# Two of four Strassen weight sums moved from VectorE to accumulating transfers

## The chip, the cores and the metric

One core of a Trainium2 chip runs the whole program. The metric is the device time of one execution in microseconds. The engines are TensorE (PE; its weight loads are listed apart as PEld), VectorE (DVE), ScalarE (ACT), GpSimd (POOL) and SyncE (SP). SP and POOL also issue transfers; in this kernel SP issues nearly all of them.

## The reference

Two decoder layers over 512 tokens of width 2048, all in float32. Layer A selects keys with an indexer and attends to them; layer B is stick-breaking attention over one shared K and V. Each mixer's output is gated, projected, added to the residual, normalised, and gets a gated per-layer embedding. What the change touches are two products at the start of layer B, the shared K/V and the queries:

```
def shared_kv(x, w_kv):
    b, s, _ = x.shape
    k, v = jnp.split(x @ w_kv, [KVW_B], axis=-1)
    return k.reshape(b, s, N_KV_B, HEAD_DIM), v.reshape(b, s, N_KV_B, HEAD_DIM)

def mixer_b(x, w_in, w_o, k, v):
    b, s, _ = x.shape
    q, gate = jnp.split(x @ w_in, [WIDTH_B], axis=-1)
    ...
    o = from_blocks(lax.map(block_fn, (to_blocks(q), starts)))
    return (o * jax.nn.silu(gate)) @ w_o
```

## The kernel before

Activations lie transposed, as 16 blocks of 128 rows by 512 tokens. Every matrix product runs on values split in two: a high part rounded by ScalarE (`XH`, `wh`, `sh`) and the rest, formed by VectorE (`XL`, `wl`, `sl`), so a product of two blocks is three matmuls (`mm3`, lines 134 to 136).

Weights stream through a ring of three `raw` tiles of 128 x 2 x 512. `units` lists every load in the order of use; `next_raw` fills the ring from SP and hands out the oldest tile. A tile is free again when the last split has read it. `Ahead(..., 2)` keeps the split parts two items ahead of TensorE, and `wh` and `wl` have three buffers each. K of layer B is a plain product (`kitems`, eight units of two k blocks, in order `PAIRS`). V and the four groups of queries are five Strassen products in Winograd's form (`strassen_items`, `gemm_s`, lines 325 to 389): each job halves the width (256 columns), the inner dimension (1024) and the tokens (256) and needs seven products. One unit is k block k and k block k + 8, and eight units make a job, so 40 units in all. Call the four quarters of a unit q0 (upper left), q1 (upper right), q2 (lower left), q3 (lower right). VectorE forms in `st` four sums of them:

```
s1 = q0 + q2
s2 = s1 - q1
s3 = q1 - q0
s4 = q3 - s2
```

Then for each half of 128 columns the three quarters q1 to q3 and the four sums are split (128 x 384 and 128 x 512), and one item of seven pairs goes to TensorE: 21 matmuls of 256 columns. When a job's seven products are complete, `combine` (the last job: `combine_last`) adds them up from PSUM into the four quarters of the output while the next job runs in the banks that come free. During the plain product for K, `first_chunk` builds the activation sums for Strassen and the plain splits of the activations (`xl`), and at its last k block calls `stream().prime()`, which prepares the first two Strassen items.

TensorE's instructions stay in the order of the code. The other engines' order is set by a scheduler with a simulated timeline, but each engine takes its own queue in order: an instruction that waits holds up all behind it. `paced` and `pinned` mark instructions that the scheduler must leave in program order.

In the names of the rows, `raw` is a loaded weight tile, `wh` and `wl` (and `sh`, `sl`) the split weights, `st` the weight sums, `xh` and `xl` split activations, `c3h` and `c3l` split activation sums, `E` and `f` storage for activations, `u` and `m` a combine's helper tile and the product banks.

Of the kernel before, what the change touches and what calls it, by code (L numbers as in the profile page):

```python
# [77 lines left out]
def trunk_kernel(  # L78
# [85 lines left out]
    def add_job(src, c0, n=512, nk=NK, strassen=False):  # L164
        if n <= 128:
            units.extend((src.rearrange("(k p) n -> p k n", p=128)[:, k : k + 8, c0 : c0 + n],) for k in (0, 8))
            return
        step = nk // 2
        for k in range(step):
            a, b = (k, k + step) if strassen else (2 * k, 2 * k + 1)  # L170
            units.append((src, a, b, c0, n))
# [4 lines left out]

    def next_raw():
        while sent[0] < len(units) and len(raws) < 3:
            raw = top.tile([128, 2, 512], F32, name="raw", tag="raw", bufs=3)
            unit = units[sent[0]]  # L180
            if len(unit) == 1:
# [42 lines left out]
    def weight_parts():  # L224
        return tuple(top.tile([128, 512], F32R, name=n, tag=n, bufs=3) for n in ("wh", "wl"))
# [99 lines left out]
    def strassen_items(widths, wp):  # L325
        units = [n for n in widths for _ in range(NK // 2)]

        def prepare(n):
            raw = next_raw()
            rows = n // 256  # L330
            q = raw.rearrange("p a (b n) -> p (a b) n", b=2)
            two = [q[:, i].rearrange("p (j c) -> p j c", j=rows) for i in range(4)]
            st = wp.tile([128, 4 * H], F32, name="st", tag="st", bufs=2)[:, : 2 * n]
            st = st.rearrange("p (j i c) -> p j i c", j=rows, i=4)
            dve.tensor_tensor(st[:, :, 0], two[0], two[2], ALU.add)
            dve.tensor_tensor(st[:, :, 2], two[1], two[0], ALU.subtract)
            return q, two, st

        ready = prepare(units[0])
        for u, n in enumerate(units, 1):  # L340
            q, two, st = ready
            s1, s2, s3, s4 = (st[:, :, i] for i in range(4))
            dve.tensor_tensor(s2, s1, two[1], ALU.subtract)
            dve.tensor_tensor(s4, two[3], s2, ALU.subtract)
            rows = n // 256
            for j in range(rows):
                wh = top.tile([128, 512], F32R, name="wh", tag="wh", bufs=3)
                wl = top.tile([128, 512], F32R, name="wl", tag="wl", bufs=3)
                sh = wp.tile([128, 4, 128], F32R, name="sh", tag="sh", bufs=3)
                sl = wp.tile([128, 4, 128], F32R, name="sl", tag="sl", bufs=3)  # L350
                qh, ql = (w.rearrange("p (b c) -> p b c", b=4)[:, 0:3] for w in (wh, wl))
                split(qh, ql, q[:, 1:4, j * 128 : (j + 1) * 128])
                split(sh, sl, st[:, j])
                if j == rows - 1 and u < len(units):
                    ready = prepare(units[u])
                yield [(qh[:, i], ql[:, i]) for i in range(3)] + [(sh[:, i], sl[:, i]) for i in range(4)]
# [31 lines left out]
    def combine(wp, M, dst):  # L388
# [9 lines left out]
        dve.tensor_tensor(u, m6, u, ALU.add)  # L398
        pinned[0] = False

        def onto(c):
            dve.tensor_tensor(c, c, u, ALU.add)

        def rest():
            dve.tensor_tensor(c22, c12, c21, ALU.add)
            dve.tensor_tensor(c12, m3, c12, ALU.add)
            dve.tensor_tensor(c21, c21, m4, ALU.subtract)

        paced(rest)
        return [lambda c=c: onto(c) for c in (c12, c21, c22)]  # L410

    def combine_last(wp, M, dst):
# [6 lines left out]
        for out, a, b, op in (  # L419
            (c11, m2, u, ALU.add),  # L420
            (u, m6, u, ALU.add),
# [911 lines left out]
```

## Time and profile before

| | us |
|---|---|
| median of 3 runs | 1889.02 (1888.74 to 1889.87) |
| span of the profiled execution, first to last instruction | 1886.3 |
| own time of the profiled execution beside its span | not listed by the page; the median of the runs is 2.7 above the span |
| Strassen stage, first to last of its matmuls | 1037 to 1242 |
| granted TensorE clock, mean | 0.999 |

The page lists, for each engine, busy time, share of the span and number of instructions; then groups of instructions by line, with mean nanoseconds of one and the idle time of the engine before them; then the waits by the instruction that ended them. Rows of single instructions give the start and the duration in us from the span's start; a bracket at their end gives the engine's idle time before and what ended it. A line L111 or L134 is that of a helper, so groups are told apart by their tiles.

### The profile page before, as it was taken

How to read it: one execution, taken by the hardware profiler on the slowest of the kernel's cores; microseconds unless marked ns; L12 is line 12 of the kernel's file. 1: busy time of each engine (PE TensorE's matmuls, PEld its weight loads, DVE VectorE, ACT ScalarE, POOL GpSimd, SP SyncE). 2: the span in 40 equal slices, each digit the busy share in tenths (PEclk: the TensorE clock that was granted, in tenths of full speed). 3: DMA queues.
4: the chain of work that ended last, by engine and by line, in shares of the span. 5: the costliest groups of instructions: out<-in, count | busy, mean ns of one | idle time of the engine just before them, and what ended most of it. 6: DMA issues, size and time to landing. Idle time of an engine off the chain costs nothing.

```text
span 1886.3 us, 25050 instructions
## 1 busy us (share of the span) xinstructions
PE 1872.6 (99%) x9229; PEld 1586.7 (84%) x9229; DVE 1218.9 (65%) x2384; ACT 928.1 (49%) x1690; POOL 28.4 (2%) x49
## 2 busy tenths in 40 slices
PE   9999999999999999999999999999999999999998
PEld 8898888888888888888888999988888888888887
DVE  5668879966556454675368788866656645567534
ACT  4446323355554432474245444468877743347422
POOL 0000000000000000000000000000100000000000
PEclk9999999999999999999999999999999999999999
DMA  6432333312222432333343333322122153242333
GB/s 185 137 115 64 101 91 99 101 56 68 67 68 60 162 114 78 123 101 103 121 130 116 103 100 113 102 90 72 63 68 68 60 186 100 74 129 89 123 101 112
DMA packets 110587, 189.22 MB, mean 100 GB/s; under 512 B 8240, under 2 KB 28208, under 8 KB 110464
## 3 DMA queue, kind: packets, MB, share of 16 engines
q1 hardware_dynamic: 110320, 187.33, 32.4%
q8 instruction: 72, 1.18, 0.3%
q14 instruction: 51, 0.42, 0.1%
q0 software_dynamic: 144, 0.30, 0.1%
HBM read 179.21 MB, written 8.39 MB: 99 GB/s over the span
## 4 chain that ended last, share of the span: by engine, by line
PE 96%; DVE 2%; ACT 1%; DMA 1%; issue 0%; SPq 0%; POOL 0%; DVEq 0%; POOLq 0%
PE g L134 12%; PE g L135 12%; PE g L136 12%; PE o L135 7%; PE o L134 7%; PE o L136 7%; PE m L134 3%; PE m L135 3%; PE m L136 3%; PE q L136 3%; PE q L134 3%; PE q L135 3%; PE z L1214 2%; PE k L136 2%; PE k L135 2%; PE k L134 2%
## 5 line engine op out<-in xcount | busy, mean ns | idle before, releaser
L111 ACT ACTIVATE wh<-raw 128x512 fp32r<-128x512 f32 (+3 forms) x684 | 396.4, 581 | 674.4 <-PE g L135 239.4
L111 DVE TENSOR_TENSOR wl<-raw,wh 128x512 fp32r<-128x512 f32 (+3 forms) x684 | 429.6, 629 | 429.9 <-ACT wh L111 415.1
L134 PE MATMUL g<-xh,wh 128*128 128x512 f32 x1024 | 403.9, 394 | 0.2
L135 PE MATMUL g<-xl,wh 128*128 128x512 f32 x1024 | 400.3, 391 | 0.6 <-DVE xl L111 0.6
L136 PE MATMUL g<-xh,wl 128*128 128x512 f32 x1024 | 399.9, 390 | 0.0
L134 PEld LDWEIGHTS g<-xh,wh 128*128 128x128 f32 x1024 | 192.8, 188 | 40.4 <-ACT sg L111 1.9
L136 PEld LDWEIGHTS g<-xh,wl 128*128 128x128 f32 x1024 | 192.3, 188 | 40.8
L135 PEld LDWEIGHTS g<-xl,wh 128*128 128x128 f32 x1024 | 192.5, 188 | 38.4 <-DVE xl L111 1.4
L136 PE MATMUL o<-xh,wl 128*128 128x512 f32 x512 | 199.4, 389 | 0.1
L134 PE MATMUL o<-xh,wh 128*128 128x512 f32 x512 | 199.2, 389 | 0.0
L135 PE MATMUL o<-xl,wh 128*128 128x512 f32 x512 | 199.2, 389 | 0.0
L136 PEld LDWEIGHTS o<-xh,wl 128*128 128x128 f32 x512 | 96.1, 188 | 20.6 <-DVE wl L111 0.7
L134 PEld LDWEIGHTS o<-xh,wh 128*128 128x128 f32 x512 | 96.1, 188 | 20.2 <-ACT wh L111 0.2
L135 PEld LDWEIGHTS o<-xl,wh 128*128 128x128 f32 x512 | 96.1, 188 | 20.0
L134 PE MATMUL q<-xh,wh 128*128 128x512 f32 x256 | 99.6, 389 | 0.0
L135 PE MATMUL q<-xl,wh 128*128 128x512 f32 x256 | 99.6, 389 | 0.0
L136 PE MATMUL q<-xh,wl 128*128 128x512 f32 x256 | 99.6, 389 | 0.0
L111 ACT ACTIVATE sh<-st 128x512 fp32r<-128x512 f32 x80 | 49.0, 628 | 79.7 <-PE m L135 42.5
L111 DVE TENSOR_TENSOR sl<-st,sh 128x512 fp32r<-128x512 f32 x80 | 54.4, 689 | 37.2 <-ACT sh L111 37.2
L111 DVE TENSOR_TENSOR xl<-f,xh 128x512 fp32r<-128x512 f32 x80 | 54.3, 686 | 11.4 <-ACT f L111 11.0
L111 ACT ACTIVATE wk<-z 128x512 f32<-128x512 f32 x80 | 47.1, 590 | 25.7 <-PE z L136 18.0
L135 PEld LDWEIGHTS q<-xl,wh 128*128 128x128 f32 x256 | 48.1, 188 | 10.0
(290 smaller groups left out, 3366.5 us busy)
## 6 DMA issues: line engine op xcount, KB each, us to landing
raw<-w_in_a SPq DMA_DIRECT2D x95, 512.0 KB, 3.7
raw<-w_in_b SPq DMA_DIRECT2D x64, 512.0 KB, 3.8
raw<-w_ple_gate SPq DMA_DIRECT2D x52, 512.0 KB, 3.7
raw<-w_o_a SPq DMA_DIRECT2D x24, 512.0 KB, 3.9
raw<-w_o_b SPq DMA_DIRECT2D x24, 512.0 KB, 3.8
raw<-w_kv_b SPq DMA_DIRECT2D x16, 512.0 KB, 3.8
raw<-w_ple_gate SPq DMA_DIRECT2D x24, 256.0 KB, 2.9
f<-xT SPq DMA_DIRECT2D x4, 1024.0 KB, 6.4
```

The source lines that it names most:

```text
L111: ins = method(*args, **kw)
L134: pe.matmul(out, a[0], b[0], start=start, stop=False)
L135: pe.matmul(out, a[0], b[1], start=False, stop=False)
L136: pe.matmul(out, a[1], b[0], start=False, stop=stop)
L1214: pe.matmul(z, m, p, start=False, stop=n == len(terms), skip_group_check=True)
```

## The change

A Strassen load is now a unit of its own kind, `(src, k, c0)`, which `load_sums` brings in by five transfers into a `raw` tile of 128 x 5 x 256. SP loads q0 twice, into slots 0 and 1, by one broadcast transfer, then q2 and q3 into slots 3 and 4, and q1 into slot 2. POOL then adds q1 onto slot 0 and q2 onto slot 1, by transfers that accumulate in the tile. So slot 0 is q0 + q1 and slot 1 is q0 + q2. Only additions are used: two of the seven operands and with them the products' combination change sign (`combine`, `combine_last`). VectorE still forms two sums, slot 1 + q1 and q3 + that. The split is dealt out anew: 128 x 640 from the tile (five slots), 128 x 256 from `st` (two sums). The ring has four `raw` tiles, and the list of K's plain units is written out since `add_job(..., strassen=True)` now makes the new kind. The scratch that POOL's transfers reserve is set to 4096 bytes per partition.

```
@@ add_job
+            if strassen:
+                units.append((src, k, c0))
+            else:
+                units.append((src, 2 * k, 2 * k + 1, c0, n))
@@
+    def load_sums(raw, src, k, c0):
+
+        rows = src.rearrange("(k p) n -> p k n", p=128)
+        left, right = slice(c0, c0 + 256), slice(c0 + 256, c0 + 512)
+        nc.sync.dma_start(raw[:, 0:2], rows[:, k : k + 1, left].broadcast_to([128, 2, 256]))
+        both = raw[:, 3:5].rearrange("p a n -> p (a n)")
+        nc.sync.dma_start(both, rows[:, k + 8, c0 : c0 + 512])
+        nc.sync.dma_start(raw[:, 2], rows[:, k, right])
+        pool.dma_start(raw[:, 0], rows[:, k, right], accum_op=ALU.add)
+        pool.dma_start(raw[:, 1], rows[:, k + 8, left], accum_op=ALU.add)
@@ next_raw
-        while sent[0] < len(units) and len(raws) < 3:
-            raw = top.tile([128, 2, 512], F32, name="raw", tag="raw", bufs=3)
+        while sent[0] < len(units) and len(raws) < 4:
+            raw = top.tile([128, 5, 256], F32, name="raw", tag="raw", bufs=4)
             unit = units[sent[0]]
+            if len(unit) == 3:
+                load_sums(raw, *unit)
+                raws.append(raw)
+                sent[0] += 1
+                continue
@@ strassen_items
-            dve.tensor_tensor(st[:, :, 0], two[0], two[2], ALU.add)
-            dve.tensor_tensor(st[:, :, 2], two[1], two[0], ALU.subtract)
...
-            dve.tensor_tensor(s2, s1, two[1], ALU.subtract)
-            dve.tensor_tensor(s4, two[3], s2, ALU.subtract)
...
+            st = wp.tile([128, 2, 256], F32, name="st", tag="st", bufs=2)
+            dve.tensor_tensor(st[:, 0], raw[:, 1], raw[:, 2], ALU.add)
+            return raw, st
+
+        ready = prepare()
+        for u in range(len(widths) * NK // 2 - 1, -1, -1):
+            raw, st = ready
+            dve.tensor_tensor(st[:, 1], raw[:, 4], st[:, 0], ALU.add)
+            for j in range(2):
+                cols = slice(j * 128, (j + 1) * 128)
+                q = tuple(w.rearrange("p (b c) -> p b c", b=5) for w in weight_parts(640))
+                t = tuple(wp.tile([128, 2, 128], F32R, name=n, tag=n, bufs=3) for n in ("sh", "sl"))
+                split(*q, raw[:, :, cols])
+                split(*t, st[:, :, cols])
+                if j and u:
+                    ready = prepare()
+                s3, s1, a11, a22, a12 = ((q[0][:, i], q[1][:, i]) for i in range(5))
+                s2, s4 = ((t[0][:, i], t[1][:, i]) for i in range(2))
+                yield a11, a22, a12, s1, s2, s3, s4
@@ combine
-        dve.tensor_tensor(u, m6, u, ALU.add)
+        dve.tensor_tensor(u, m6, u, ALU.subtract)
...
-            dve.tensor_tensor(c22, c12, c21, ALU.add)
-            dve.tensor_tensor(c12, m3, c12, ALU.add)
-            dve.tensor_tensor(c21, c21, m4, ALU.subtract)
+            dve.tensor_tensor(c22, c12, c21, ALU.subtract)
+            dve.tensor_tensor(c12, m3, c12, ALU.subtract)
+            dve.tensor_tensor(c21, m4, c21, ALU.add)
@@
-    add_job(w_kv_b, 0, strassen=True)
+    units.extend((w_kv_b, k, k + 8, 0, 512) for k in range(8))
@@
-    nc = _bacc.Bacc("TRN2", target_bir_lowering=False, num_devices=1)
+    nc = _bacc.Bacc("TRN2", target_bir_lowering=False, num_devices=1, dynamic_dma_scratch_size=4096)
```

The change also moves instructions, since the scheduler sets them anew. First VectorE's queue at the entry to the Strassen stage, while TensorE still works on K's last k blocks. Before (`wl` of 512 columns are K's last plain splits, `st<-raw` the first sums of a unit):

```order
L111 TENSOR_TENSOR wl<-raw,wh 128x512
L111 TENSOR_TENSOR st<-raw 128x2x128 x2
L111 TENSOR_TENSOR st<-st,raw 128x2x128
L111 TENSOR_TENSOR st<-raw,st 128x2x128
L111 TENSOR_TENSOR wl<-raw,wh 128x512
L111 TENSOR_TENSOR xl_94<-E_5554,xh_78 128x256
L111 TENSOR_TENSOR xl_97<-f_107,xh_81 128x512
L111 TENSOR_TENSOR xl_105<-f_109,xh_89 128x512
L111 TENSOR_TENSOR sl<-st,sh 128x512 x2
L111 TENSOR_TENSOR wl<-raw,wh 128x512
L111 TENSOR_TENSOR st<-raw 128x2x128 x2
```

Two rows on, in that queue, comes the first Strassen split (`wl` of 384 columns), and only after it the third unit's sums. The same place in the changed kernel, up to the first Strassen splits (`wl` of 640 columns):

```order
L111 TENSOR_TENSOR st<-raw 128x256
L111 TENSOR_TENSOR wl<-raw,wh 128x512
L111 TENSOR_TENSOR st<-raw,st 128x256
L111 TENSOR_TENSOR sl<-st,sh 128x256 x2
L111 TENSOR_TENSOR wl<-raw,wh 128x512
...
L111 TENSOR_TENSOR st<-raw 128x256
L111 TENSOR_TENSOR xl_105<-f_109,xh_89 128x512
L111 TENSOR_TENSOR wl<-raw,wh 128x512 x2
...
L111 TENSOR_TENSOR st<-raw 128x256
L111 TENSOR_TENSOR st<-raw,st 128x256
L111 TENSOR_TENSOR wl<-raw,wh 128x640 x2
```

The first sum (`st<-raw`) now stands ahead of the plain split that was before it (k block 12), and the first Strassen splits stand behind the third unit's first sum and the second unit's second sum.

Second, VectorE at the first change of job, where `combine` (into `E`, through `u`) frees the banks that TensorE's next products need. Before:

```order
L111 TENSOR_TENSOR wl<-raw,wh 128x384
L111 TENSOR_TENSOR st<-raw 128x2x128 x2
L111 TENSOR_TENSOR E_5554<-m_8866,u 128x2x256
L111 TENSOR_TENSOR st<-st,raw 128x2x128
L111 TENSOR_TENSOR u<-m_8867,u 128x512
```

And in the changed kernel:

```order
L111 TENSOR_TENSOR wl<-raw,wh 128x640
L111 TENSOR_TENSOR st<-raw,st 128x256
L111 TENSOR_TENSOR E_5556<-m_8885,u 128x2x256
L111 TENSOR_TENSOR u<-m_8886,u 128x512
L111 TENSOR_TENSOR E_5556<-E_5556 128x2x256
```

One sum instead of two stands right ahead of the first bank's addition, and none between the first and the second.

Third, POOL between the masks of layer A's scores (`am`; `trf` is a constant) and those of layer B (`wk`, `run`). Before:

```order
L622 AFFINE_SELECT trf<-trf 128x128
L701 AFFINE_SELECT am_124<-am_124 128x128
L701 AFFINE_SELECT am_125<-am_125 128x128
L701 AFFINE_SELECT am_126<-am_126 128x128
L1172 AFFINE_SELECT wk<-wk 128x512 x4
L1172 AFFINE_SELECT run<-run 128x512
```

In the changed kernel the transfers stand there, two for each of the 40 units:

```order
L710 AFFINE_SELECT am1_124<-am1_124 128x128
L710 AFFINE_SELECT am2_125<-am2_125 128x128
L710 AFFINE_SELECT am3_126<-am3_126 128x128
L187 DMA raw_8691<-w_kv_b 128x256
L188 DMA raw_8691<-w_kv_b 128x256
L187 DMA raw_8735<-w_kv_b 128x256
L188 DMA raw_8735<-w_kv_b 128x256
```

The first of each pair waits until SP's broadcast transfer of its tile has landed, and the next unit's pair waits behind it in POOL's queue.

More of the change, by code (lines that the diff above doesn't have):

```diff
@@ L169, in add_job @@
         for k in range(step):
-            a, b = (k, k + step) if strassen else (2 * k, 2 * k + 1)
-            units.append((src, a, b, c0, n))
+            if strassen:
+                units.append((src, k, c0))
+            else:
+                units.append((src, 2 * k, 2 * k + 1, c0, n))
     raws = deque()
@@ L222, in __next__, with weight_parts @@
             return self.waiting.popleft()
-    def weight_parts():
-        return tuple(top.tile([128, 512], F32R, name=n, tag=n, bufs=3) for n in ("wh", "wl"))
+    def weight_parts(n=512):
+        return tuple(top.tile([128, n], F32R, name=n_, tag=n_, bufs=3) for n_ in ("wh", "wl"))
     def plain_items(jobs):
@@ L325, in strassen_items, with prepare @@
     def strassen_items(widths, wp):
-        units = [n for n in widths for _ in range(NK // 2)]
-        def prepare(n):
+        def prepare():
             raw = next_raw()
[L330 to L334, printed above, removed]
-            dve.tensor_tensor(st[:, :, 0], two[0], two[2], ALU.add)
-            dve.tensor_tensor(st[:, :, 2], two[1], two[0], ALU.subtract)
-            return q, two, st
@@ L339, in strassen_items @@
[L339 to L342, printed above, removed]
-            dve.tensor_tensor(s2, s1, two[1], ALU.subtract)
-            dve.tensor_tensor(s4, two[3], s2, ALU.subtract)
[L345 to L356, printed above, removed]
+            st = wp.tile([128, 2, 256], F32, name="st", tag="st", bufs=2)
@@ L397, in combine, with onto @@
         dve.tensor_tensor(c11, m2, u, ALU.add)
-        dve.tensor_tensor(u, m6, u, ALU.add)
+        dve.tensor_tensor(u, m6, u, ALU.subtract)
         pinned[0] = False
-        def onto(c):
-            dve.tensor_tensor(c, c, u, ALU.add)
+        def onto(c, a, b, op):
+            dve.tensor_tensor(c, a, b, op)
         def rest():
-            dve.tensor_tensor(c22, c12, c21, ALU.add)
-            dve.tensor_tensor(c12, m3, c12, ALU.add)
-            dve.tensor_tensor(c21, c21, m4, ALU.subtract)
+            dve.tensor_tensor(c22, c12, c21, ALU.subtract)
+            dve.tensor_tensor(c12, m3, c12, ALU.subtract)
+            dve.tensor_tensor(c21, m4, c21, ALU.add)
         paced(rest)
-        return [lambda c=c: onto(c) for c in (c12, c21, c22)]
+        last = ((c12, c12, u, ALU.subtract), (c21, u, c21, ALU.subtract), (c22, c22, u, ALU.add))
+        return [lambda ops=ops: onto(*ops) for ops in last]
     def combine_last(wp, M, dst):
@@ L420, in combine_last @@
             (c11, m2, u, ALU.add),
-            (u, m6, u, ALU.add),
-            (c21, m7, u, ALU.add),
+            (u, m6, u, ALU.subtract),
+            (c21, u, m7, ALU.subtract),
             (c22, m5, c21, ALU.add),
             (c12, m5, u, ALU.add),
-            (c12, m3, c12, ALU.add),
+            (c12, m3, c12, ALU.subtract),
             (c21, c21, m4, ALU.subtract),
```

## The prediction

> **What bounds the kernel.** I read the page's header, its busy line and its chain first: they say which engine sets the end.
>
> ```profile
> span 1886.3 us, 25050 instructions
> PE 1872.6 (99%) x9229; PEld 1586.7 (84%) x9229; DVE 1218.9 (65%) x2384; ACT 928.1 (49%) x1690; POOL 28.4 (2%) x49
> PE 96%; DVE 2%; ACT 1%; DMA 1%; issue 0%; SPq 0%; POOL 0%; DVEq 0%; POOLq 0%
> ```
>
> TensorE is busy 1872.6 of 1886.3 us, so all that any change off TensorE can give back is 13.7 us. The change leaves the list of matmuls alone (their shapes, operands' widths and order stay), so its worth is what it does to these gaps. Next, the table of stretches over the Strassen stage, and the waits of TensorE's weight loads inside it.
>
> ```profile
> core 0: us, PE busy (x) PEld busy (x) DVE busy (x) ACT busy (x) POOL busy (x), PEclk, DMA share, GB/s
> 1036.90:1242.00 205.10, 204.22 (x1687) 202.52 (x1687) 160.75 (x342) 92.17 (x177) 0.00 (x0) 1.00 0.34 104
> PEld m L134 <- DVE f L111: 1.1, 3, 0.4
> PEld m L134 <- DVE u L111: 1.0, 4, 0.3
> PEld m L134 <- DVE E L111: 0.4, 1, 0.4
> ```
>
> The stage runs at a granted clock of 1.00 and TensorE is idle 205.10 - 204.22 = 0.88 us in it. VectorE, which the change relieves, is busy 160.75 us of 205.10, or 78%: it is not the bound. TensorE's only waits here are on combine's instructions at the four changes of job. 40 units share the stage, so one unit of weights lasts 205.1 / 40 = 5.13 us.
>
> **What is removed.** Per unit VectorE formed four sums of 128x256; two remain.
>
> ```profile
> L111 DVE TENSOR_TENSOR st<-raw 128x256 f32<-128x256 f32 x80 | 30.2, 419 | 4.3 <-DMA raw<-w_kv_b 4.2
> L111 DVE TENSOR_TENSOR st<-raw,st 128x256 f32<-128x256 f32 x40 | 16.9, 422 | 0.8
> L111 DVE TENSOR_TENSOR st<-st,raw 128x256 f32<-128x256 f32 x40 | 16.7, 418 | 0.0
> ```
>
> 160 sums cost 30.2 + 16.9 + 16.7 = 63.8 us; 80 go, so 80 x 0.42 = 33.6 us leave VectorE, and its share of the stage falls to about (160.75 - 33) / 205 = 62%. The splits are only dealt out differently: per half unit 128x384 + 128x512 before, 128x640 + 128x256 after, 896 columns both times.
>
> ```profile
> L111 DVE TENSOR_TENSOR wl<-raw,wh 128x384 fp32r<-128x384 f32 (+1 forms) x81 | 44.7, 555 | 6.3 <-ACT wh L111 6.3
> L111 DVE TENSOR_TENSOR sl<-st,sh 128x512 fp32r<-128x512 f32 x78 | 53.1, 689 | 37.2 <-ACT sh L111 37.2
> ```
>
> 128 columns more cost 0.689 - 0.555 = 0.134 us, so I estimate the 640-wide split at 0.82 us: 0.82 + 0.42 = 1.24 against 0.555 + 0.689 = 1.24. ScalarE's copies keep their columns too. The combining instructions change signs and operand order, not number or size. All of this lies under TensorE. The one piece of it on the path is at the job changes, where VectorE reaches combine with fewer sums queued ahead: of the 0.88 us I take half, -0.4 us; the ends are 0 and -0.9.
>
> **What is added: transfers.** Per unit SP issued one 512 KB load; now it issues three (256, 256, 128 KB), and POOL two accumulating ones of 128 KB. Issues first. An SP issue takes 0.37 us (rows below), so 1.1 us per 5.13 us unit, and what is queued behind on SP is the next unit's load, which has to wait for its buffer anyway. POOL has no work at all in the stage (0.00 above), and its next instruction after the scores of layer A waits over a thousand microseconds, so nothing queues behind the two issues of 0.55 to 0.71 us.
>
> ```profile
> POOL wk L1172 <- DVE wk L111: 1155.3, 7, 1063.1
> 1.35 0.71 POOL L141 DMA_DIRECT2D lnc<-ln_c  x1 [0.34 <-issue]
> 2.04 0.55 POOL L582 DMA_DIRECT2D rc<-rope_c  x1
> ```
>
> Bandwidth: 512 KB per unit makes a DMA share of 0.34. The plain 640 KB would make 0.34 x 640/512 = 0.43. The accumulating 256 KB would add 0.17 at the price of a plain byte, and 0.34 at twice that (the destination is read as well), so 0.60 to 0.77. The engines fill up only if an accumulated byte costs over (1 - 0.43) / 0.17 = 3.4 plain ones.
>
> **What is added: a longer way from a free buffer to its first sum.** This decides. No row shows an accumulating transfer; the nearest in the list of issues (KB each, median us from issue to landing) are:
>
> ```profile
> raw<-w_kv_b SPq DMA_DIRECT2D x16, 512.0 KB, 3.8
> raw<-w_ple_gate SPq DMA_DIRECT2D x24, 256.0 KB, 2.9
> posi<-pos POOLq DMA_DIRECT2D x1, 256.0 KB, 5.5
> lnc<-ln_c POOLq DMA_DIRECT2D x1, 32.0 KB, 3.0
> rc<-rope_c POOLq DMA_DIRECT2D x1, 2.0 KB, 4.2
> ```
>
> Call L the time from a buffer's release until the second accumulation has landed: 2.9 (SP's 256 KB) + 0.71 (POOL's first issue) + the landing of the second. For that I take 4.2, the middle of POOL's three rows, since 128 KB lies between 32 and 256: L = 7.8 us. The low end takes 3.0 (L = 6.6). The high end takes twice 5.5, as if destination and source were read one after the other (L = 14.6). Before, release to sum was 3.7: the rows below show a `wl` ending at 1019.93 and the sum starting at 1023.58.
>
> [...]
>
> In the steady stage this is covered. With four buffers a freed one is wanted three units later, 3 x 5.13 = 15.4 us, against 2 x 5.13 = 10.3 us with three. L = 7.8 leaves 7.6 us; even 14.6 fits. The tight place is the entry, where VectorE takes its instructions in order and a sum that waits for its transfer holds up splits that TensorE needs.
>
> ```profile
> 1015.01 0.68 DVE L111 TENSOR_TENSOR wl<-raw,wh 128x512 fp32r<-128x512 f32 x1
> 1015.72 0.37 SPq L198 DMA_DIRECT2D raw<-w_kv_b  x1
> 1019.24 0.68 DVE L111 TENSOR_TENSOR wl<-raw,wh 128x512 fp32r<-128x512 f32 x1
> 1019.96 0.37 SPq L198 DMA_DIRECT2D raw<-w_kv_b  x1
> 1021.48 0.69 DVE L111 TENSOR_TENSOR wl<-raw,wh 128x512 fp32r<-128x512 f32 x1
> 1023.58 0.76 DVE L111 TENSOR_TENSOR st<-raw 128x256 f32<-128x256 f32 x2 [1.41 <-DMA raw<-w_kv_b]
> 1032.25 0.56 DVE L111 TENSOR_TENSOR wl<-raw,wh 128x384 fp32r<-128x384 f32 x1 [0.39 <-ACT wh L111]
> 1034.89 0.76 DVE L111 TENSOR_TENSOR st<-raw 128x256 f32<-128x256 f32 x2 [2.08 <-DMA raw<-w_kv_b]
> 1037.16 0.28 PE L134 MATMUL m<-xh,wh 128*128 128x256 f32 x1
> L134 PE MATMUL k<-xh,wh x64: 389/389/389, 993.6 to 1036.5; 128*128 128x512 f32 x64
> ```
>
> Before, the first unit's load went out at 1019.96, on the release of its third-last predecessor; with four buffers it goes out one unit of the plain job earlier, at 1015.7. That is a lead of 4.3 us, against L - 3.7 = 4.1 us more to wait: the two cancel. Now follow the changed order on VectorE. The first sum can run at 1015.7 + L, which is 1023.5 (before: 1023.58). Behind it stand the plain splits `wl` of k blocks 12 and 13. TensorE begins block n at 993.6 + 2.72 n (64 groups to 1036.5), so at 1026.2 and 1028.9; the splits are done about 1.0 and 3.6 us after the sum starts, at 1024.5 and 1027.1. The second of them frees the third unit's buffer, whose sum runs at 1015.7 + L + 3.6 + L = 1034.9. That is where it ran before (1034.89), but then the first Strassen split was already through, at 1032.25; in the new order it stands behind this sum and one more. It ends 1.6 us later (0.34 + 0.42 + 0.82), at 1036.5. TensorE wants its low part in its third matmul, at 1037.4. The margin is 0.9 us, and the entry stalls by 1020.9 + 2L - 1037.4 = 2L - 16.5 us if that is positive: from L = 8.25 on, twice, since two transfers stand one behind the other. At L = 7.8 it is 0; at 6.6 it is 0; at 14.6 it is 12.7 us.
>
> **Other moves.** The fourth buffer lets every load of the kernel start earlier, and ScalarE's and VectorE's orders shift in places. TensorE's waits show what that could touch:
>
> ```profile
> PE z L1214 <- ACT sh L111: 3.7, 1, 3.7
> PE spun L156 <- DVE xl L111: 2.0, 1, 2.0
> ```
>
> The 3.7 us after the stage hang on ScalarE's queue, whose order there is the same in both kernels; the 2.0 us are the start, before any load matters. I put 0 on both, with 1.5 us either way for small shifts.
>
> **Sum.** The page gives the span and no other time of the profiled execution; the median of the runs, 1889.02, lies 2.7 us above the span, and I keep that. 1886.3 - 0.4 + 0 + 0 = 1885.9 us of span, or 1888.6 us. A change under 0.2% (3.8 us) I count as no change; the three runs spread by 1.1.
>
> **Rivals.** *Late accumulations at the entry* (slower): VectorE in order behind a sum whose accumulation lands late. It passes 0.2% when 2L - 16.5 - 0.4 is over 3.8, so from L = 10.4, a landing over 6.8 us after issue. For it: no accumulating transfer has been timed, and POOL's 256 KB took 5.5. Against it: that one ran beside SP's first loads, and half the bytes go here. At the high end: 1889.0 + 12.7 - 0.4 = 1901.3 us. Chance 13%.
>
> [...] Chance of a decisive one 3%. [...]
>
> *Transfers become the bound* (slower): at five plain bytes for an accumulated one the share is 0.43 + 0.85 = 1.28, the stage 28% or 57 us longer, about 1946 us. For it only that the price is unknown. Chance 4%.
>
> *A true gain*: over 3.8 us would need the 3.7 us wait to vanish with all of the 0.88, or the shifts in order to remove what I do not see: 1885 or below. Chance 5%. That the sums stay on VectorE is excluded by the orders: 80 rows fewer there, 80 transfers on POOL.
>
> **How the numbers follow.** No change 75%, at 1888.6 us, by itself within 1886.5 and 1892.8; slower 13 + 3 + 4 = 20%; faster 5%. The range runs from 1886.5, which leaves the faster cases below it, to 1898, which takes in the entry's stall up to L = 13 (2 x 13 - 16.5 - 0.4 = 9.1 above 1889.0) and leaves about a third of the first slow rival and the whole of the third outside: some 15% in all.
>
> **What would show it.** Right: 80 `st` rows of about 0.42 us on VectorE, busy near 128 us in the stage; the POOL transfers land in 3 to 5 us; the stage stays at 205 us with TensorE's idle under 1 us. Wrong: a wait of TensorE on `wl` or `wh` at about 1037 (entry), a DMA share near 1 with a longer stage (bandwidth), POOL issues well over 0.7 us (descriptors), or a wait of TensorE at another place that the new orders made.

## The result and the profile after

The changed kernel takes 1903.99 us (median of four runs, 1901.61 to 1914.65) against 1888.88 before (four runs, 1887.65 to 1889.87): ratio 1.0093, 95% interval 1.0077 to 1.0109. It is slower by 0.9%, and outside the predicted range (1886.5 to 1898). Its profiled execution took 1904.58 us and has a span of 1902.9, 16.6 us more than before.

The page of the changed kernel, header, busy line and chain:

```profile
span 1902.9 us, 25428 instructions
PE 1878.7 (99%) x9229; PEld 1591.1 (84%) x9229; DVE 1193.9 (63%) x2304; ACT 932.5 (49%) x1690; POOL 97.8 (5%) x129
PE 91%; DMA 4%; DVE 3%; ACT 1%; issue 1%; POOL 0%; SPq 0%; DVEq 0%; ACTq 0%; POOLq 0%
```

TensorE has the same 9229 matmuls and is busy 6.1 us longer, a first sign of a slower clock (the mean granted clock of the profiled execution is 0.996, before 0.999). VectorE lost 80 instructions as planned. The chain now runs through transfers for 4% of the span, where it was 1%. I divide the 16.6 us by two marks on TensorE, the first and the last matmul into `m`: the first moved from 1037.16 to 1040.43 (3.3 us, all before the stage), the last from 1243.26 to 1259.56, so the stage grew from 206.1 to 219.1 us (13.0), and 0.3 us came behind it.

The stage as a stretch, from its first to its last matmul into `m`, and 40 us of it, from the table of stretches of the changed kernel:

```profile
core 0: us, PE busy (x) PEld busy (x) DVE busy (x) ACT busy (x) POOL busy (x), PEclk, DMA share, GB/s
1040.43:1259.68 219.25, 209.86 (x1697) 206.79 (x1696) 140.74 (x272) 97.26 (x178) 62.48 (x72) 0.98 0.71 163
1080.00:1120.00 40.00, 35.30 (x271) 35.01 (x271) 24.78 (x47) 15.89 (x30) 12.14 (x14) 0.91 0.66 148
```

TensorE is idle 219.25 - 209.86 = 9.4 us in the stage instead of 0.88, which is 8.5 us of the 13.0. The other 4.5 us are busy time: the same matmuls took 205.34 us before (the line is shown with e16). Half of the idle time, 4.7 us, lies in one stretch of 40 us, and there the mean clock is down to 0.91; 9% of 40 us makes an estimated 3.6 of the 4.5 us. Who waits for whom, from the lists of waits (total, times, longest):

```profile
DVE st L111 <- DMA raw<-w_in_b: 38.0, 12, 5.4
DVE st L111 <- DMA raw<-w_kv_b: 17.1, 4, 5.7
PE m L134 <- DVE E L111: 4.7, 1, 4.7
PE m L136 <- DVE wl L111: 3.4, 4, 2.4
PE iq L134 <- ACT wh L111: 1.8, 2, 1.6
```

VectorE waits 55.1 us in 16 places for the tile that its first sum reads. Most of that is absorbed by the two items prepared ahead; TensorE feels 4.7 us of it at a change of job, and 3.4 us at four places. One such wait in full, from the timelines of VectorE, SP and POOL in the changed kernel (start, duration, engine, line, instruction, and in brackets the idle time before and what ended it):

```profile
1042.32 1.55 DVE L111 TENSOR_TENSOR wl<-raw,wh 128x640 fp32r<-128x640 f32 x2
1043.90 0.38 SPq L183 DMA_DIRECT2D raw<-w_kv_b  x1
1047.55 0.85 POOL L187 DMA_DIRECT2D raw<-w_kv_b  x1 [7.13 <-DVE wl L111]
1048.09 1.19 POOL L188 DMA_DIRECT2D raw<-w_kv_b  x1
1048.99 0.82 DVE L111 TENSOR_TENSOR wl<-raw,wh 128x640 fp32r<-128x640 f32 x1 [0.31 <-ACT wh L111]
1054.89 0.43 DVE L111 TENSOR_TENSOR st<-raw 128x256 f32<-128x256 f32 x1 [3.69 <-DMA raw<-w_kv_b]
1055.24 0.82 DVE L111 TENSOR_TENSOR wl<-raw,wh 128x640 fp32r<-128x640 f32 x1
```

The two splits of the first unit free its buffer at 1043.87. SP loads at once (1043.90), and POOL can add 3.65 us later (1047.55); the bracket of that row names VectorE's split, but this had ended by then, and what POOL still needed was SP's broadcast. The second addition goes out at 1048.09 and has landed 6.8 us later (1054.89). L is 11.0 us here. The sum that wants the tile belongs to the fifth unit, and it stands directly ahead of the *third* unit's second split (1055.24). The next such wait, from the same timelines:

```profile
1056.08 0.38 SPq L183 DMA_DIRECT2D raw<-w_kv_b  x1
1059.91 1.17 POOL L188 DMA_DIRECT2D raw<-w_kv_b  x1
1065.30 0.43 DVE L111 TENSOR_TENSOR st<-raw 128x256 f32<-128x256 f32 x1 [3.70 <-DMA raw<-w_kv_b]
```

Here L is 9.2 us, of which the second addition's landing takes 5.4. And one further on, at the first change of job, from the timelines of VectorE and TensorE:

```profile
1087.94 0.43 DVE L111 TENSOR_TENSOR st<-raw 128x256 f32<-128x256 f32 x1 [5.35 <-DMA raw<-w_in_b]
1088.28 0.82 DVE L111 TENSOR_TENSOR wl<-raw,wh 128x640 fp32r<-128x640 f32 x1
1089.35 0.68 DVE L111 TENSOR_TENSOR E<-m,u 128x512 f32<-128x512 f32 x1
1090.09 0.58 PE L134 MATMUL m<-c3h,sh 128*128 128x256 f32 x1 [4.70 <-DVE E L111]
1090.47 0.41 PE L135 MATMUL m<-c3l,sh 128*128 128x256 f32 x1
```

Here `combine` stands behind the waiting sum, so TensorE loses 4.7 us, and its next matmuls last 0.41 us instead of 0.28: the granted clock, in stretches of 1 us, is 1.00 up to 1089, 0.75 in the next, still in the idle time, and 0.50 from 1090 to 1096.

The start. The fourth entry of SP's timeline, and the stretches from 5 to 15 us, in the kernel before:

```profile
7.46 0.38 SPq L198 DMA_DIRECT2D raw<-xT  x1
```

```profile
5.00:10.00 5.00, 4.66 (x16) 3.70 (x17) 2.42 (x4) 1.14 (x2) 0.07 (x1) 1.00 0.88 251
10.00:15.00 5.00, 5.00 (x26) 4.38 (x25) 3.24 (x6) 2.78 (x6) 0.00 (x0) 1.00 0.80 236
```

The same in the changed kernel:

```profile
3.13 0.47 SPq L216 DMA_DIRECT2D raw<-xT  x1
```

```profile
5.00:10.00 5.00, 3.47 (x12) 2.92 (x12) 1.81 (x3) 0.57 (x2) 0.07 (x1) 1.00 0.97 289
10.00:15.00 5.00, 4.68 (x15) 4.25 (x16) 3.67 (x7) 3.09 (x6) 0.00 (x0) 0.66 0.69 230
```

With a fourth buffer the fourth load goes out at 3.13 and shares the transfers' throughput (0.97 of it) with the two loads that TensorE waits for; TensorE does 12 matmuls instead of 16 there. After its wait of 1.6 us the clock is lower too: 5 us at a mean of 0.66 cost an estimated 1.7 us, and the two together are the 3.3 us.

### The profile page after: what moved, and what is told of

It reads as the page before. It is cut to its first block, busy times and chain, and to the rows that moved or that the text cites. A ratio compares the mean times of both kernels' runs of the same rounds, so it can differ in the third digit from the quotient of the medians.

```text
span 1902.9 us, 25428 instructions
## 1 busy us (share of the span) xinstructions
PE 1878.7 (99%) x9229; PEld 1591.1 (84%) x9229; DVE 1193.9 (63%) x2304; ACT 932.5 (49%) x1690; POOL 97.8 (5%) x129
## 3 DMA queue, kind: packets, MB, share of 16 engines
q0 software_dynamic: 11664, 10.79, 3.8%
## 4 chain that ended last, share of the span: by engine, by line
PE 91%; DMA 4%; DVE 3%; ACT 1%; issue 1%; POOL 0%; SPq 0%; DVEq 0%; ACTq 0%; POOLq 0%
PE g L135 12%; PE g L134 12%; PE g L136 12%; PE o L135 7%; PE o L134 7%; PE o L136 7%; PE q L136 3%; PE q L135 3%; PE q L134 3%; PE m L136 2%; PE m L134 2%; PE m L135 2%; DMA raw<-w_in_b 2%; PE z L1223 2%; DMA raw<-w_kv_b 1%; PE iq L136 1%
## 5 line engine op out<-in xcount | busy, mean ns | idle before, releaser
L111 ACT ACTIVATE wh<-raw 128x512 fp32r<-128x512 f32 (+3 forms) x684 | 414.6, 607 | 673.4 <-PE g L135 239.3
L111 DVE TENSOR_TENSOR wl<-raw,wh 128x512 fp32r<-128x512 f32 (+3 forms) x684 | 451.4, 661 | 437.6 <-ACT wh L111 421.9
L111 ACT ACTIVATE sh<-st 128x256 fp32r<-128x256 f32 x80 | 32.7, 415 | 96.3 <-PE m L135 78.9
L136 PE MATMUL m<-xh,wl 128*128 128x256 f32 x240 | 69.0, 288 | 3.6 <-DVE wl L111 3.4
L134 PE MATMUL m<-xh,wh 128*128 128x256 f32 x240 | 68.5, 286 | 0.0
L135 PE MATMUL m<-xl,wh 128*128 128x256 f32 x240 | 68.2, 284 | 0.0
```

The lines of the kernel that those rows point to most:

```text
L111: ins = method(*args, **kw)
L134: pe.matmul(out, a[0], b[0], start=start, stop=False)
L135: pe.matmul(out, a[0], b[1], start=False, stop=False)
L136: pe.matmul(out, a[1], b[0], start=False, stop=stop)
```

## The experiments

My theory after these profiles: two separate losses. The start's is the fourth load. The stage's comes from the order on VectorE: the scheduler put each first sum one unit earlier than the code has it, so that the transfers' lead is one unit shorter. Rivals: the transfers' throughput, an accumulating transfer that disturbs the engines, and POOL's issues. Each run below stands beside runs of the kernel before, whose median was 1888.5 to 1888.7 us each time.

| run | what | us | ratio, 95% |
|---|---|---|---|
| e1_pin | first sum in program order | 1891.32 | 1.0012 [1.0004, 1.0021] |
| e2_late4 | a limit of three loads at first | 1904.65 | 1.0081 [1.0068, 1.0094] |
| e3_before4 | before, with four buffers | 1891.27 | 1.0014 [1.0005, 1.0023] |
| e4_plain | no accumulation | 1890.27 | 1.0006 [0.9997, 1.0015] |
| e5_swap | additions in the other order | 1894.54 | 1.0031 [1.0022, 1.0040] |
| e12_pin_swap | both of e1 and e5 | 1890.03 | 1.0009 [1.0000, 1.0018] |
| e13_before4_late | e3, fourth load held back | 1889.49 | 1.0006 [0.9997, 1.0015] |
| e15_pin_late | e1, fourth load held back | 1889.00 | 1.0002 [0.9993, 1.0011] |
| e14_pin_swap_late | e12, fourth load held back | 1889.08 | 1.0003 [0.9994, 1.0011] |
| e16_before_fill | before, a wait filled | 1887.66 | 0.9995 [0.9986, 1.0004] |
| e17_late_fill | e14, the same wait filled | 1886.47 | 0.9988 [0.9979, 0.9996] |

### e1_pin: the first sum in program order

```diff
-            dve.tensor_tensor(st[:, 0], raw[:, 1], raw[:, 2], ALU.add)
+            paced(dve.tensor_tensor, st[:, 0], raw[:, 1], raw[:, 2], ALU.add)
```

> The changed kernel, with the first sum of each unit (st[:, 0]) kept behind the VectorE instruction written before it. In VectorE's queue it then stands five half units after the release of the buffer that its load uses, instead of three. Theory 'order' (VectorE reaches the sum 7.7 us after the release, L is 10 to 11 us, so the queue stalls every other unit): lead becomes 12.8 us, the waits of VectorE on raw in the stage fall from 55 us to under 15, TensorE idles under 2 us in the stage, 1891 to 1893 us. Theory 'transfers too slow' (the stage is held by the transfers' rate, DMA share 0.72): VectorE waits as long at the later place, 1899 us or more. The start keeps its 3.2 us by both.

Measured 1891.32. The stage from its first to its last matmul, from the table of stretches of this run:

```profile
1040.78:1244.28 203.50, 203.50 (x1698) 203.35 (x1696) 139.62 (x268) 95.38 (x178) 62.45 (x72) 1.00 0.74 175
```

TensorE has no idle time left, at no smaller a DMA share (0.74 for 0.71) and with the same bytes, and VectorE's list of waits has no row on `raw` in this stage any more. Time, idle time and waits are as the theory of order had it. One word of order takes back all of the stage's loss, while the transfers, their throughput and POOL's work are those of the changed kernel. This is the run that fells the rivals for the stage. What remains over before is the start (its first matmul into `m` at 1040.78).

### e4_plain: the same transfers without the addition

```diff
-        pool.dma_start(raw[:, 0], rows[:, k, right], accum_op=ALU.add)
-        pool.dma_start(raw[:, 1], rows[:, k + 8, left], accum_op=ALU.add)
+        pool.dma_start(raw[:, 0], rows[:, k, right])
+        pool.dma_start(raw[:, 1], rows[:, k + 8, left])
```

Slots 0 and 1 then hold q1 and q2 alone, not the sums. VectorE's order is that of the changed kernel.

> The changed kernel, with POOL's two transfers per unit as plain copies over the slots: the additions are left out, so slots 0 and 1 hold q1 and q2. Same instructions in the same order on every engine. Theory 'adding costs' (reading the destination as well doubles the landing): the second transfer lands in 3 us or less after its issue instead of 5 to 6, L under 8.5, DMA share in the stage 0.60 instead of 0.72, total 1893 to 1897. Theory 'order' with a latency that is POOL's path and not the addition: landing within 0.7 us of that with addition, 1901 to 1904.

Measured 1890.27, which is 2.7 us under the range of the theory 'adding costs' and far from its rival's. The software queue (packets, MB, share of the engines' time) and POOL's transfers (KB, median us to landing), of the changed kernel and then of this run:

```profile
q0 software_dynamic: 11664, 10.79, 3.8%
raw<-w_in_b POOLq DMA_DIRECT2D x64, 128.0 KB, 3.9
raw<-w_kv_b POOLq DMA_DIRECT2D x16, 128.0 KB, 5.0
```

```profile
q0 software_dynamic: 3984, 10.79, 1.9%
raw<-w_in_b POOLq DMA_DIRECT2D x64, 128.0 KB, 2.4
raw<-w_kv_b POOLq DMA_DIRECT2D x16, 128.0 KB, 2.5
```

The same bytes in a third of the packets, in half the engines' time, landing in 2.4 to 2.5 us. The stage lasts 204.5 us, at a DMA share of 0.56 (0.60 expected). With L shorter by that, the same shortened lead suffices: the loss in the stage needs both, the early place of the sum and the long way of the accumulation. By itself this run would also fit a limit of throughput, since the share of the transfers fell with the landing; that is excluded by e1, at a share of 0.74. An accumulating transfer lands, by the rows above, 1.5 to 2.5 us later than a plain one.

### e5_swap: the additions in the other order

```diff
-        pool.dma_start(raw[:, 0], rows[:, k, right], accum_op=ALU.add)
         pool.dma_start(raw[:, 1], rows[:, k + 8, left], accum_op=ALU.add)
+        pool.dma_start(raw[:, 0], rows[:, k, right], accum_op=ALU.add)
```

> The two additions are issued in the other order: slot 1, which the first sum reads, before slot 0. VectorE's order is as in the changed kernel. Order theory: the first sum of a unit stands directly ahead of the second 640-wide remainder of the unit two earlier, so two units last at least L plus some 1.2 us, and the stage loses 8 times what L + 1.2 is above 10.26 us (L = 10.9 gives 14.8 us; 13.1 were lost). The transfer that is waited for is issued one POOL issue (0.54 to 0.85 us) earlier and shares less time with its sister, so L falls by 0.5 to 1.5 us and the time by 4 to 12 us: 1896 us, range 1892 to 1900, and VectorE's waits on raw become short. Rival, the transfers' throughput bounds the stage: the bytes and the packets are the same, 1903 to 1904 us.

Measured 1894.54, inside the range. VectorE's and TensorE's waits in this run:

```profile
DVE st L111 <- DMA raw<-w_in_b: 18.9, 11, 3.5
DVE st L111 <- DMA raw<-w_kv_b: 10.3, 5, 5.8
PE m L134 <- DVE E L111: 2.0, 1, 2.0
PE m L136 <- DVE wl L111: 1.2, 1, 1.2
```

VectorE's waits fall from 55.1 to 29.2 us, TensorE's two from 8.1 to 3.2, the stage from 219.1 to 211.0. The bytes are the same, so throughput is excluded a second time; what counts is when the one slot lands that the sum reads. My formula (8 times the excess of L) was too even, though: the losses sit at the stage's entry and at the change of job, with a lower clock there (a mean of 0.96 from 1080 to 1120 us), and not in each pair of units.

### e2_late4 and e3_before4: the start

```diff
-        while sent[0] < len(units) and len(raws) < 4:
+        while sent[0] < len(units) and len(raws) < (3 if sent[0] < 24 else 4):
```

> The changed kernel, with at most three loads under way for the first 24 loads and four after that. Theory 'fourth load at the start' (the fourth 512 KB load goes out at 3.13 us and delays the load that TensorE waits for from 8.2 to 9.5 us, and the idle time lowers the clock): the first 3.2 us of the loss vanish, 1900 to 1901.5 us, first matmul of the Strassen stage at 1037.2 instead of 1040.4. Rival (that start is chance of one profile): 1903 to 1905.

Measured 1904.65, as the rival had it, but this is no answer: SP still issued the fourth load at 3.13. That count bounds how far the code runs ahead, while the scheduler starts a load as soon as one of the four buffers is free. e3 is the kernel before with four `raw` tiles and four loads ahead, and with the scratch of 4096 bytes (that line is not shown):

```diff
-        while sent[0] < len(units) and len(raws) < 3:
-            raw = top.tile([128, 2, 512], F32, name="raw", tag="raw", bufs=3)
+        while sent[0] < len(units) and len(raws) < 4:
+            raw = top.tile([128, 2, 512], F32, name="raw", tag="raw", bufs=4)
```

> The kernel before, with four raw tiles and four loads under way and 4096 bytes of scratch; nothing else. Theory 'fourth load at the start': 3 us slower than before, 1891.5 to 1892.5, lost before 20 us. Rival (the start's loss comes from the POOL transfers or the scratch or is chance): 1888 to 1890. If the fourth buffer gave something elsewhere, the loss at the start would stay and the end be less late.

Measured 1891.27, 2.6 us over before, just under the expected range and well above the rival's, without any accumulating transfer. Its stage lasts 206.1 us as before, so the loss lies elsewhere, and the profile shows it at the start: TensorE's wait there was 0.2 us before and is now, by the list of waits:

```profile
PE iq L134 <- ACT wh L111: 1.3, 1, 1.3
```

This profile is of the fastest of the 11 executions (1889.71 us), and K's first matmul stands only 1.4 us later in it than before (995.0 against 993.6).

### Five runs with named buffers, which don't test the start

To keep the fourth buffer out of use until unit 27 I named the four tiles and used them by number.

```diff
+    ring = [top.tile([128, 5, 256], F32, name=f"raw{i}") for i in range(4)]
...
+            if sent[0] == 27:
+                paced(dve.memset, ring[3][:, 0, :1], 0.0)
-            raw = top.tile([128, 5, 256], F32, name="raw", tag="raw", bufs=4)
+            raw = ring[sent[0] % (3 if sent[0] < 24 else 4)]
```

> The four buffers are named tiles used by number, and only three are in use until unit 27, so the fourth load at the very start is gone; the order of VectorE in the Strassen stage is the changed kernel's. Theory of two separate losses: the start's 3 us come back, the stage's 13 us stay: 1900.8 us (1900 to 1901.5). Rival, the start's delay is due to something else: 1903.5 to 1904.5 us.

> Both repairs: the first sum kept in program order, and the fourth buffer out of use until unit 27. Theory of two separate losses: nothing is left of them, and 1891.3 less 2.6 us is 1888.7 us (1887.8 to 1889.5), no difference from before although VectorE does 80 sums less: the stage is TensorE's. Rival, the accumulating transfers cost something by themselves (TensorE or VectorE slowed by the DMA traffic): 1890.5 to 1892 us.

> As the run with both repairs, and the additions issued in the other order. Theory: once L is covered by the order, its length is worth nothing within the stage, and at most some 1 us at the entry of the stage, where TensorE's first matmul stood at 1040.8 us with the pin alone and 1037.16 before (some 3 us of which are the start's): 1888.5 us (1887.5 to 1889.3), the same as with both repairs. Rival, L still ends the stage's first wait: 0.5 to 1.5 us faster than the run with both repairs.

They took 1909.35, 1898.81 and 1897.18 us, all far above what was expected. In the code's order a load can now come ahead of a reader of the buffer's former contents, so some products are formed from other data and the waits are other ones; these times don't test the start. In two more, with `len(raws) < (3 if sent[0] < 27 else 4)`, some products are still formed from other data, at a place that was not found:

> Both repairs with the loads ahead counted right: the first sum kept in program order, and of the four named buffers three in use, with at most three loads ahead, until unit 27. Theory of two separate losses: the stage is TensorE's as with the pin alone, and the start's 2.6 us come back: 1888.7 us (1887.8 to 1889.5), the first wait on iq back at about 0.2 us. Rival, the pin's 2.6 us over before are a cost of the accumulating transfers: 1890.5 to 1892 us.

> As the run with both repairs, and the two additions issued in the other order (slot 1, which the first sum reads, first). Theory: with the order repaired the length of L is worth nothing within the stage and at most 1 us at its entry: 0 to 1 us below the run with both repairs, 1888.3 us (1887.3 to 1889.2). Rival, the transfers' length is still paid in each unit: 2 us or more below it.

They took 1894.53 and 1894.24 us, again far above. Within the first group the order of the sums (10.5 us between the first two) and of the additions (1.6 us) acts as in e1 and e12; the 0.3 us of the second group are within the scatter. More is not taken from these times.

### e12, e13, e15, e14: the fourth load held back

e12 joins the edits of e1 and e5:

> The changed kernel with its own four rotating buffers, the first sum kept in program order and the additions issued in the other order. Theory: the stage's entry alone can gain from the earlier landing (first matmul of the stage at 1040.8 us with the pin alone, of which some 3 us are the start's): 1890.9 us (1890.0 to 1891.5), the start's loss remains (first wait on iq 1.5 to 2.5 us).

Measured 1890.03, at the low end of its range (the first wait on iq was 1.2 us, 1.5 to 2.5 expected). Then the fourth load was held back in a way that leaves the rotating buffers alone: one column of the second load is copied into the fourth tile first.

```diff
             raw = top.tile([128, 5, 256], F32, name="raw", tag="raw", bufs=4)
+            if sent[0] == 3:
+                dve.tensor_copy(raw[:, 0, :1], raws[1][:, 1, 511:512])
```

In the kernel before with four buffers (e13), in e1 (e15) and in e12 (e14):

> The kernel before with four buffers (1891.3 us), and the fourth load at the very start made to wait for the first two, by a copy of one column. Theory that the fourth load at the start costs the 2.6 us: back to the kernel before, 1888.7 us (1888.2 to 1889.3), first wait on iq 0.2 to 0.5 us. Rival, the fourth buffer costs its time elsewhere: 1891 us.

> As the run before it with the additions in the changed kernel's order. Theory: 1891.3 us less 2.6: 1888.7 us (1888.0 to 1889.5), no difference from before. Rival, the rest is a cost of the accumulating transfers: 1891 us.

> The changed kernel with the first sum in program order, the additions issued in the other order, and the fourth load at the start held back. Theory: 1890.0 us less 2.6: 1887.5 us (1886.8 to 1888.5), faster than before by up to 0.1%, the first wait on iq 0.2 to 0.5 us and the stage TensorE's alone. Rival, the rest is a cost of the accumulating transfers: 1890 us.

Measured 1889.49, 1889.00 and 1889.08: 1.8, 2.3 and 1.0 us less than without it, and none differs from before beyond its interval. Only e15 lies in its range: e13 is 0.2 us above its own, and e14, which was to be faster than before, 0.6 us. From SP's timeline of e15, and from the list of waits of e13:

```profile
8.50 0.38 SPq L218 DMA_DIRECT2D raw<-xT  x1
```

```profile
PE iq L134 <- ACT wh L111: 0.2, 1, 0.2
```

In all three the time falls, so the fourth load at the start was a good part of what remained; the scratch, which e13 keeps, can account for the rest at most. But that one wait doesn't measure it: it is 0.9 us in e14, where 0.2 to 0.5 was expected, and 1.0 in e15. K's first matmul is a better mark. It stands at 993.6 us in the kernel before and at 992.6 in e16 (below), at 994.4 to 994.7 in the four profiles that hold the load back (e13, e14, e15, e17), and at 994.2 to 997.3 in the seven that don't. The three latest of these seven (996.8 to 997.3: the changed kernel, e1 and e2) are the ones with a mean clock of 0.97 over the first 50 us; in e3 and e4 it is 1.00 there, and in e5 and e12 from 5 to 40 us. So in these profiles 1 to 2 us of the start stay in the repaired kernels, and what holding the load back saves seems to be above all the clock. The mean granted clock of all executions says the same: 0.99782 in e3 and 0.99855 in e13, 0.99664 in e1 and 0.99745 in e15, 0.99709 in e12 and 0.99736 in e14. Over 1888 us the differences are an estimated 1.4, 1.5 and 0.5 us.

### e16 and e17: where the stage's gain went

With the order repaired the stage is not as long as before but shorter: 203.4 us against 206.1, by the starts of its first and last matmul. From the tables of stretches, first of the kernel before, then of e14, each from the first to the last matmul into `m`, with the same 1698 matmuls:

```profile
1037.16:1243.38 206.22, 205.34 (x1698) 203.71 (x1697) 161.77 (x343) 93.25 (x178) 0.00 (x0) 1.00 0.34 103
```

```profile
1037.95:1241.44 203.49, 203.49 (x1698) 203.34 (x1696) 139.62 (x268) 95.60 (x178) 62.47 (x72) 1.00 0.74 175
```

2.7 us are gained, yet the time is the same as before. Behind the stage stands the 3.7 us wait of the first softmax operand, and behind that a low clock. Stretches of 4 us after the wait, of the kernel before and then of e14:

```profile
1263.38:1267.38 4.00, 3.31 (x7) 2.29 (x8) 3.77 (x6) 3.30 (x7) 0.18 (x1) 0.57 0.40 147
1267.38:1271.38 4.00, 4.00 (x19) 3.26 (x19) 2.34 (x5) 3.40 (x7) 0.52 (x1) 1.00 0.00 0
```

```profile
1261.44:1265.44 4.00, 3.09 (x6) 1.64 (x6) 2.97 (x5) 3.29 (x7) 0.62 (x1) 0.62 0.37 142
1265.44:1269.44 4.00, 3.73 (x9) 2.68 (x9) 1.76 (x3) 1.26 (x4) 0.02 (x1) 0.53 0.01 2
```

In us at a clock of 0.50, added up over stretches of 1 us: 3.4 in the profiles of before, of the changed kernel and of e3, 6.8 in e4, e5, e13, e14 and e15, 10.2 in e1 and e12. The rest of the program behind the stage is longer too: 643.0 us before, 645.4 in e14, 646.2 in e1. Half of the longer half clock makes an estimated 1.7 of the 2.4 us in e14, and 3.4 us, where 3.2 were lost, in e1. The three lengths are once, twice and three times 3.4 us; why is not shown. Nor does the length of a wait alone decide: the clock was also lower after shorter waits of TensorE, of 1.6, 1.7 and 2.2 us at the start (the changed kernel, e2 and e1, each with a mean of 0.97 over the first 50 us) and of 2.0 us at a change of job (e5, 0.96 over 40 us). After the 2.4 us at the entry to the changed kernel's stage it was 1.00, and e17, with a wait of 1.5 us at its start, has a mean of 1.000 over its whole profiled execution.

The test: 16 matmuls of 128 x 512 into an unused bank fill the wait, in the kernel before (e16) and in e14 (e17); their result is not used.

```diff
+                if not g and s == 1 and fn == weights:
+                    fill = bank(7, "fill")
+                    for _ in range(16):
+                        pe.matmul(fill, XL[15][:, :128], XL[15], start=True, stop=True)
```

> The kernel before, with 16 matmuls of 128x512 into an unused PSUM bank (16 x 0.227 = 3.6 us) in TensorE's 3.7 us wait for the first softmax operand; their result is not used. Theory that the half clock (3.3 us at 0.50) follows from the wait: the wait becomes busy, the half clock goes, 1.65 us gained: 1886.9 us (1886.3 to 1887.7). Rival, the half clock has another cause: no change, 1888.5 us, or up to 0.3 us slower.

> The changed kernel with all repairs (first sum in program order, additions in the other order, fourth load at the start held back), and the same 16 matmuls in that wait. Theory that the stage's gain of 2.7 us was given back by a longer half clock (6.6 us at 0.50, so 3.3 us lost): 1889.1 less 3.3 is 1885.8 us, and 1 to 2 us below the kernel before with the same filling, with which it then shares all but the stage (203.4 for 206.1 us) and the start (0.8 us later): 1885.0 us (1884.3 to 1886.5). Rival, the profiles' length of the half clock is chance and the runs' medians don't hold the stage's gain: the same as the kernel before with the filling within 0.5 us.

Measured 1887.66 and 1886.47. The ten microseconds after the wait in e17, and its stage:

```profile
1260.00:1270.00 10.00, 9.39 (x39) 6.81 (x38) 6.62 (x11) 8.99 (x19) 1.68 (x3) 1.00 0.30 102
1038.02:1241.51 203.49, 203.49 (x1698) 203.34 (x1697) 139.61 (x268) 95.59 (x178) 63.21 (x73) 1.00 0.75 175
```

The clock stays at 1.00, and what follows the stage lasts 643.1 us in both runs. e17 is 2.0 us faster than before (0.9988, 0.9979 to 0.9996), the only version that beats both kernels beyond its interval, by 0.1%. For the transfers alone the fair comparison is with e16, which has the same filling: 1.2 us, for which there is no interval on record. That is less than the stage's 2.7 us because the part ahead of the stage is longer: the first matmul into `m` stands 1.9 us later in e17 than in e16, at 1038.02 against 1036.11. And e16's gain (0.8 us, 1.65 expected) is inside its interval, and its part behind the stage is no shorter than before's (643.1 against 643.0), so in that kernel the filling cost about what the clock gave.

That the stage's gain goes into the clock holds for all executions, not only for one profile of each. The mean granted clock is 0.9985 over the 27 executions of the kernel before that stand beside e14, 0.9974 over e14's 11, 0.9997 over e16's and 0.9999 over e17's. Of 1887 us that makes an estimated 2.8, 5.0, 0.5 and 0.2 us, so e14 loses 2.2 us more to the clock than before, most of the 2.7. Why the low clock lasts longer there is not shown.

## Why the prediction was wrong, step by step

**"In the steady stage this is covered ... 3 x 5.13 = 15.4 us": the step that failed.** It counted the buffers and not the queue. A buffer comes free with the second split of unit n; the first sum of unit n + 4 stands, in the queue that ran, directly ahead of the second split of unit n + 2. That is two units later, 10.26 us, less one split (0.82) and the sum's own place (0.35): 9.1 us. In two of the runs with named buffers (e6 and e7) the rows of VectorE's order carry the buffer's number (119, 120, 121, 122, in the order of the units), so that it can be read. Without the pin (e6), the sum is that of two units on:

```
L111 TENSOR_TENSOR wl<-raw_120,wh 128x640
L111 TENSOR_TENSOR sl<-st,sh 128x256
L111 TENSOR_TENSOR st<-raw_122 128x256
L111 TENSOR_TENSOR wl<-raw_120,wh 128x640
L111 TENSOR_TENSOR st<-raw_122,st 128x256
```

With it (e7), that of the next unit, which leaves a whole unit more:

```
L111 TENSOR_TENSOR wl<-raw_120,wh 128x640
L111 TENSOR_TENSOR sl<-st,sh 128x256
L111 TENSOR_TENSOR st<-raw_121 128x256
L111 TENSOR_TENSOR wl<-raw_120,wh 128x640
L111 TENSOR_TENSOR st<-raw_121,st 128x256
```

The head of the stage in the changed kernel already showed it: the third unit's first sum stands ahead of any 640-wide split. Those rows stand in the section on the change, and the prediction used them for the entry alone. With L between 9.2 and 11.0 the lead is missed by up to 2 us, the two items ahead run dry, and the first stall that reaches TensorE at a job change costs 4.7 us and then the clock (0.91 over the 40 us there).

**L.** Put at 7.8 us (6.6 to 14.6), measured 9.2 to 11.0. Two of its three terms were low: SP's broadcast took 3.3 to 3.6 us (2.9) and the second addition's landing 5.4 to 6.8 (4.2). The third was not: POOL's second issue starts 0.54 to 0.58 us after the first (0.71). Even 11.0 would have fitted into the 15.4 us, so it is the lead that decides.

**The entry.** The mechanism and the condition were right. In the changed kernel two loads stand one behind the other there, from 1018.97 to 1028.73 us (9.8) and from 1032.12 to 1041.52 (9.4). With these, 2L - 16.5 becomes 9.8 + 9.4 - 16.5 = 2.7 us, and TensorE's longest wait on a low part, which is the one at the entry, was 2.4. It alone would have made 1891.

**"I put 0 on both, with 1.5 us either way": the second failed term.** The fourth buffer costs 2.6 us (e3, median) and, with the clock after the wait, 3.3 in the changed kernel's profile, at the start and by a load that comes too early, not late.

**Held.** TensorE's list of matmuls is the same; the sums that left took time off TensorE at most at the job changes; the DMA share in the stage is 0.71 to 0.75 (0.60 to 0.77), and an accumulated byte costs two plain ones (3.8% against 1.9% of the engines' time, the changed kernel and e4), as assumed; the 3.7 us wait stayed. VectorE is busy 139.6 us in the undisturbed stage, not near 128: 161.8 - 139.6 = 22.2 us less, since the rows of sums in a row overlap (two of 0.42 us show as one row of 0.76 at 1023.58 in the kernel before) and their durations don't add up. The job changes gave 2.7 us in the repaired kernels, where 0.4 was put: 0.88 of idle and 1.85 that show as busy time of the same 1698 matmuls (205.34 against 203.49).

**The rivals.** The nearest was *late accumulations*: the right mechanism, at the entry only, decisive from L = 10.4. It came in the whole stage, where the prediction had excluded it. Throughput is excluded by e1 and e5. A hold-up of POOL's issues by VectorE, for which the prediction has 3%, is shown by no run, and it is not needed: the landing took 6.8 us at 1048.09 while VectorE was idle for 3.7 us of it. The prediction's sign for that rival, issues on POOL well over 0.7 us, did come (0.85 and 1.19), but in e4, with VectorE's queue as it was and plain transfers, they took 0.54, so it is the addition that lengthens them.

## What to carry to other kernels

More buffers give a transfer more lead only if the in-order engine that reads it comes to it later: count the lead in that engine's queue as scheduled, from the instruction that frees the buffer to the first one that needs the next load, and compare it with the whole chain of issues and landings (here an estimated 9.1 us against 9.2 to 11.0). A further buffer also starts a further load where the first ones are still awaited (here at 3.13 us; e3 took 2.6 us more than before). And a gain ahead of an idle time may be lost in the clock after it, as the 2.7 us of e14's stage were for the most part here (3.7 us of idle time, then 6.8 us at 0.50), so look at the granted clock there before crediting it.

## What the runs showed of the hardware

- An accumulating transfer of 128 KB makes 144 packets ((11664 - 144) / 80; the 144 are the queue's packets in the kernel before) where a plain one makes 48, takes twice the engines' time (3.8% against 1.9%), lands in 3.9 to 5.0 us instead of 2.4 to 2.5, and its two issues on POOL take 0.85 and 1.19 us instead of 0.54 each (the changed kernel and e4).
- After the idle time of 3.7 us behind the stage TensorE ran at a clock of 0.50 for 3.4, 6.8 or 10.2 us; filled with matmuls, the same place kept 1.00 (e16, e17). After waits of 1.6, 2.2, 1.7 and 2.0 us (the changed kernel, e1, e2, e5) the mean clock was 0.66 over 5 us, 0.66 over 5 us, 0.97 over 50 us and 0.96 over 40 us, an estimated 3 to 3.4 us at 0.50 each time, while it was 1.00 after one of 2.4 us (the changed kernel, 1037 to 1050).
- Waits of TensorE of 0.2 to 0.4 us at the job changes cost more than they show: the same 1698 matmuls were busy 205.34 us with them (before) and 203.49 without (e14). At these places matmuls start 0.32 to 0.48 us apart (before, 1078.44 to 1205.12), where 0.12 is usual.
